# An encoder layer on one core: attention's last units write the out-projection's operand directly, rows are scaled in place, and the second pass loads in order on the sync queue

## The chip, the cores and the metric

The kernel runs on one core of a Trainium2 chip. The metric is the device time of one execution in microseconds (us). Three executions of the kernel before gave 2356.87, 2357.80 and 2357.84 us; the median is 2357.8. One more execution was recorded by the profiler: it took 2354.58 us, and the span of its recorded instructions is 2352.8 us, so 1.8 us lie outside the span.

## The reference

One layer on 2048 tokens plus 16 meta tokens, width 1024, all float32:

```python
hn = rms_norm(h, g_mix)
q, k, v, u = split(hn @ w_in)                  # 4 query heads, 2 key/value heads of 128; u is 512 wide
q, k = rope(rms_norm(q, g_q)), rope(rms_norm(k, g_k))
attn = softmax(q k^T / sqrt(128)) v            # every token sees every token
four = real(fft2(u per group of 128)) @ w_fourier
h = h + concat(rms_norm(attn), rms_norm(four)) @ w_out
h = h + relu(rms_norm(h) @ w_up)^2 @ w_down    # 1024 -> 4096 -> 1024
return rms_norm(h, g_final)[:, 16:]
```

## The kernel before

**Precision.** Every product of float32 matrices is made from three matmuls in a reduced type (`mm3`, lines 80 to 82): each operand is split into a high and a low part, high by high, high by low, low by high. A split is one cast on ACT (line 70) and one subtraction on DVE (line 71).

**Order of the work.** The program is written as generators. A scheduler turns it into one instruction order for each engine, and each engine runs its own order and waits on semaphores where an operand comes from another. The queue of SP (sync engine) and the queue of POOL (GpSimd) start the transfers, each in its own order: a transfer that has to wait holds up all that stand behind it in that queue.

**Stages.** First the in-projection, norms, rope and the first half of the Fourier transform. Then attention (about 327 to 1003 us of the span): 16 units, each 256 tokens by one key/value group with its two query heads. A unit's queries `q` are loaded by `start` (line 728) on the POOL queue, where the keys `kt` (line 704) and values `vn` (line 713) are loaded as well. A unit ends by splitting its output into `ohl` and storing the parts to the buffer `o_d` in device memory (line 853).

**Out-projection.** `out_a(b)` (from line 1009) does a block of 512 tokens: it loads the block's attention output from `o_d` into the operand `at` (line 1032), multiplies it with the weights into PSUM tiles `poa`, adds the result to the rows `h` (line 1042), squares them for the norm of the MLP (`hj`, line 1043) and stores them to `h_d` (line 1049). Four row tiles of 128 tokens make a block. Blocks 0 to 2 run in the shadow of attention, block 3 after it.

**Flip.** `flip(b)` (line 1052) makes the MLP's operand of a block: it scales the four row tiles by their norm into copies `m` (line 1057, 16 copies of 128 by 256 for a block), transposes these on TensorE into `pmt` (line 1062), applies the gain (`mt`, line 1064) and stores to `m_d`.

**MLP.** Two passes of 1024 tokens. Each pass is an up product and a down product in the seven-product scheme of Strassen and Winograd: operands are combined to seven forms, taken in the order "1265734" (`ORDER`). In the up pass one operand is `bf` (the seven forms of the tokens, which stay for the pass) and the other the weights' forms `wuh`, `wul` (`up_weights`, from line 1097), built from `R` (line 1104) for each of eight groups; a form is 24 matmuls per group. The results go through relu and square to `s_d`. In the down pass there are four groups of seven forms of 48 matmuls; tokens `ah`, `al` come from `s_d`, weights `bh`, `bl` from `w_down`. Both operands go through rings of tiles: `ar` (5 raw tiles), `a` (8), `b` (10).

**Between the stages.** After block 2 of the out-projection the program splits forms "1" and "2" of the first pass (blocks 0 and 1 of tokens), runs block 3 of the out-projection with the flip of block 2 between its parts, then the flip of block 3, then the other five forms. The second pass' forms are prepared during the first up pass (`forms_ahead`) and stored to `f_d`; they come back as seven transfers `bf<-f_d` of 2 MB (line 1536), four on POOL's queue behind the two weight loads `R`, three on SP's behind the stores of the first pass' output (line 1403).

Of the kernel before, what the change touches and what calls it, by code (L numbers as in the profile page):

```python
# [19 lines left out]
P = 128  # L20
# [6 lines left out]
NQ = 4  # L27
# [24 lines left out]
A_BUFS = 6  # L52
# [83 lines left out]
def encoder_block(ctx: ExitStack, tc: tile.TileContext, x, meta, w_in, w_f,  # L136
# [580 lines left out]
    sqs = {}  # L717

    def attention():
# [5 lines left out]
        def start(u):  # L725
            b, g = units[u]
            q = ap.tile([P, 2, 2, 256], R32, name=f"q_{u}", tag="q", bufs=2)
            nc.gpsimd.dma_start(q, q_d[b][:, :, 2 * g:2 * g + 2])
            q = q.rearrange("p l h n -> p l (h n)")
            state[u] = dict(q=(q[:, 0], q[:, 1]), S=[], k=KV["k", u])  # L730
# [107 lines left out]
        def finish(u):  # L838
# [11 lines left out]
            hl = ap2.tile([P, 2, 512], R32, name=f"ohl_{u}", tag="ohl", bufs=1)  # L850
            split(hl[:, 0], hl[:, 1], O)
            for e in range(2):
                nc.sync.dma_start(o_d[b // 2][:, e, 2 * g:2 * g + 2, c],
                                  f32v(hl[:, e]).rearrange("p (h n) -> p h n", h=2))
# [158 lines left out]
    def out_a(b):  # L1013
# [15 lines left out]
        A = ey.tile([P, 2, NQ, 512], R32, name=f"at_{b}", tag=f"e{b % 2}")  # L1029
        for k in range(NQ):  # L1030
            for e in range(2):
                nc.sync.dma_start(f32v(A[:, e, k]), o_d[b][:, e, k])
        MS[b] = ms = []
        for t in range(T):
# [14 lines left out]
            nc.sync.dma_start(h_d[2 * b0 + t], hs[t])  # L1049

    def flip(b):

        hs, ms = H.pop(b), MS.pop(b)
        for kk in range(KT // 2):
            m = [a_tile(f"m_{b}_{i}_{kk}").rearrange("p (t e) -> p t e", t=2) for i in range(2)]
            for t in range(4):
                nc.scalar.activation(m[t // 2][:, t % 2], hs[t][:, kk * 256:(kk + 1) * 256], AF.Copy, scale=ms[t])
            for i in range(2):
                k = 2 * kk + i
                ps = bank(f"pmt_{b}_{k}")  # L1060
                for t in range(4):
                    nc.tensor.transpose(ps[:, t * P:(t + 1) * P], m[t // 2][:, t % 2, i * P:(i + 1) * P], ident)
                raw = a_tile(f"mt_{b}_{k}")
                nc.scalar.activation(raw, ps, AF.Copy, scale=c_mlp(k))
                nc.sync.dma_start(m_d[b][:, k], raw)
            yield
# [30 lines left out]
    def up_weights(p, sp):  # L1097

        sp_t = {}
        for g in range(8):  # L1100
            R = []
            for i in range(2):
                r = sp.tile([P, 4, 512], F32, name=f"R{i}_{p}_{g}", tag=f"R{i}")
                (nc.gpsimd if p and not g else nc.sync).dma_start(r, w_up[i * 512:(i + 1) * 512, g * 512:(g + 1) * 512].rearrange("(k p) f -> p k f", p=P))
                R.append(r)
# [4 lines left out]
            def form(name, src):  # L1110
                hi, lo = (sp.tile([P, 4, 256], R32, name=f"wu{e}{name}_{p}_{g}", tag="wu" + e, bufs=WU_BUFS) for e in "hl")
                split(hi, lo, src)
                return hi, lo

            yield form("1", a11)
            yield form("2", a12)
# [11 lines left out]

    def bf_tile(pool, name, **kw):
        t = pool.tile([P, 2, 4, 512], R32, name="bf" + name, **kw)  # L1130
        BF[name] = [[t[:, e, k] for k in range(4)] for e in range(2)]
        return t

    def b_form(pool, name, src, **kw):

        t = bf_tile(pool, name, **kw)
        for c in (slice(0, 2), slice(2, 4)):
            split(t[:, 0, c], t[:, 1, c], src[:, c])
# [5 lines left out]
    def forms_ahead(lf):  # L1144

        for k, i in itertools.product(range(4), range(2)):
            r, c = {}, slice(i * 256, i * 256 + 256)
            for n, b, kk in (("11", 2, k), ("21", 2, k + 4), ("12", 3, k), ("22", 3, k + 4)):
                r[n] = lf.tile([P, 256], F32, name=f"lr{n}_{k}_{i}", tag="lr" + n)
                nc.sync.dma_start(r[n], m_d[b][:, kk, c])  # L1150

            def keep(name, src):
                t = lf.tile([P, 2, 256], R32, name=f"lf{name}_{k}_{i}", tag="lf", bufs=2)
                split(t[:, 0], t[:, 1], src)
                nc.sync.dma_start(f_d[name][:, :, k, c], f32v(t))

            sub = lambda d, a, b: nc.vector.tensor_tensor(r[d], r[a], r[b], op=ALU.subtract)
            keep("1", r["11"])
            yield
            keep("2", r["21"])  # L1160
            yield
            sub("11", "12", "11")
            keep("5", r["11"])
            yield
            sub("11", "22", "11")
            keep("6", r["11"])
            yield
            sub("12", "22", "12")
            keep("7", r["12"])
            yield  # L1170
            keep("3", r["22"])
            yield
            sub("21", "21", "11")
            keep("4", r["21"])
# [75 lines left out]
    def first_down(p, sp, FIRST):  # L1250

        a = sp.tile([P, 4, 512], F32, name=f"a1_{p}", tag="R0")
        nc.sync.dma_start(a, s_d[0][:, 0])
        w = sp.tile([P, 4, 512], F32, name=f"d11_{p}", tag="R1")
# [3 lines left out]
        for h in range(2):  # L1258
            for x, r in (("a", a), ("b", w)):
                tags = ("us1", "us2") if h and x == "b" else ("wuh", "wul")  # L1260
                hi, lo = (sp.tile([P, 2, 512], R32, name=f"{x}{e}1_{p}_{h}", tag=t, bufs=WU_BUFS if t in ("wuh", "wul") else 1)
                          for e, t in zip("hl", tags))
# [4 lines left out]
    def down_pass(p, sp, FIRST, hs):  # L1267
# [3 lines left out]
        for i, j in ((1, 1), (2, 1), (1, 2), (2, 2)):  # L1271
            pass
        own, RING = {}, {"a": (dn, 8)}

# [371 lines left out]
```

## Time and profile before

| what | value |
|---|---|
| median of three runs | 2357.8 us |
| the profiled execution | 2354.58 us, span 2352.8 us |
| TensorE busy (PE) | 2258.5 us, 96% of the span |
| VectorE (DVE) | 1694.7 us, 72% |
| ScalarE (ACT) | 1190.2 us, 51% |
| GpSimd (POOL) | 234.7 us, 10% |
| mean granted TensorE clock | 0.981 |
| attention | about 327 to 1003 us |
| between attention and the first up pass | about 1003 to 1115 us |
| first up pass, first down pass | to about 1387 us, to 1699 us |
| second up pass, second down pass | from 1719 to about 2044 us, to the end |

TensorE is busy in nearly all of the span, so what matters is where it is idle (about 94 us) and where its granted clock is below one. The view of waits names, for each engine, the instruction that waited and what released it; the timeline shows one wait at its place; the windows give the busy time of every engine and the granted clock for a stretch.

### The profile page before, as it was taken

How to read it: one execution, taken by the hardware profiler on the slowest of the kernel's cores; microseconds unless marked ns; L12 is line 12 of the kernel's file. 1: busy time of each engine (PE TensorE's matmuls, PEld its weight loads, DVE VectorE, ACT ScalarE, POOL GpSimd, SP SyncE). 2: the span in 40 equal slices, each digit the busy share in tenths (PEclk: the TensorE clock that was granted, in tenths of full speed). 3: DMA queues.
4: the chain of work that ended last, by engine and by line, in shares of the span. 5: the costliest groups of instructions: out<-in, count | busy, mean ns of one | idle time of the engine just before them, and what ended most of it. 6: DMA issues, size and time to landing. Idle time of an engine off the chain costs nothing.

```text
span 2352.8 us, 28180 instructions
## 1 busy us (share of the span) xinstructions
PE 2258.5 (96%) x10238; PEld 1786.2 (76%) x10238; DVE 1694.7 (72%) x2250; ACT 1190.2 (51%) x2045; POOL 234.7 (10%) x275
## 2 busy tenths in 40 slices
PE   9999989999999999967999999999879999999998
PEld 7889877766666666655888878888758888788887
DVE  5434669999998988845767659778635556597786
ACT  6333346656555657646656544324435555443244
POOL 1212120013232021100000020000100000200000
PEclk9999999999999999988999999999989999999999
DMA  6333142133343544354776486444274444864442
GB/s 205 89 91 100 54 146 78 50 121 110 112 135 119 179 130 144 134 207 148 243 245 223 167 311 217 145 149 135 99 321 170 140 156 159 304 216 147 147 135 81
DMA packets 192908, 368.47 MB, mean 157 GB/s; under 512 B 15856, under 2 KB 74864, under 8 KB 191104
## 3 DMA queue, kind: packets, MB, share of 16 engines
q1 hardware_dynamic: 172320, 304.84, 38.6%
q0 software_dynamic: 20304, 61.56, 8.0%
q8 instruction: 81, 1.33, 0.2%
q14 instruction: 59, 0.48, 0.1%
q10 hardware_dynamic: 144, 0.26, 0.0%
HBM read 236.28 MB, written 130.32 MB: 156 GB/s over the span
## 4 chain that ended last, share of the span: by engine, by line
PE 79%; DVE 7%; DMA 7%; ACT 3%; issue 2%; POOL 1%; SPq 0%; POOLq 0%; DVEq 0%; ACTq 0%
PE o L836 8%; PE dx L81 5%; PE dx L80 5%; PE dx L82 5%; PE dy L82 4%; PE dy L80 4%; PE dy L81 4%; PE ux L82 3%; PE ux L80 3%; PE ux L81 3%; PE uy L81 2%; PE uy L80 2%; PE uy L82 2%; PE s L80 2%; PE s L82 2%
## 5 line engine op out<-in xcount | busy, mean ns | idle before, releaser
L836 PE MATMUL o<-S,vn 128*128 128x512 f32 x512 | 244.2, 596 | 2.5 <-ACT S L828 1.9
L70 ACT CAST ah<-a 128x1024 fp32r<-128x1024 f32 x112 | 117.1, 1049 | 236.8 <-issue 122.8
L80 PE MATMUL ux<-bf,wuh 128*128 128x512 f32 x512 | 202.4, 395 | 29.2 <-DMA bf<-f_d 19.8
L767 ACT COPY S<-s 128x512 f32<-128x512 f32 x256 | 146.6, 585 | 111.4 <-PE s L82 91.9
L80 PE MATMUL dx<-bh,ah 128*128 128x512 f32 x512 | 200.1, 391 | 2.8 <-ACT bh L70 2.6
L81 PE MATMUL dx<-bl,ah 128*128 128x512 f32 x512 | 199.8, 390 | 2.1 <-DVE bl L71 2.1
L81 PE MATMUL ux<-bf,wuh 128*128 128x512 f32 x512 | 201.7, 394 | 0.0
L82 PE MATMUL ux<-bf,wul 128*128 128x512 f32 x512 | 201.5, 394 | 0.0
L82 PE MATMUL dx<-bh,al 128*128 128x512 f32 x512 | 199.4, 389 | 0.1
L80 PE MATMUL uy<-bf,wuh 128*128 128x512 f32 x384 | 151.1, 394 | 14.7 <-ACT bf L70 11.7
L827 DVE TENSOR_TENSOR S<-S,mb 128x1024 f32<-128x1024 f32 x128 | 155.7, 1232 | 12.0 <-ACT mb L798 11.9
L828 ACT ACTIVATE S<-S 128x1024 f32<-128x1024 f32 x128 | 135.1, 1063 | 43.7 <-DVE S L827 42.6
L80 PE MATMUL s<-q,kt 128*128 128x512 f32 (+1 forms) x272 | 146.1, 537 | 11.1 <-DMA q<-q_d 9.7
L80 PE MATMUL dy<-bh,ah 128*128 128x512 f32 (+1 forms) x388 | 151.9, 391 | 4.2 <-ACT ah L70 4.2
L71 DVE TENSOR_TENSOR al<-a,ah 128x1024 fp32r<-128x1024 f32 x112 | 136.2, 1223 | 25.9 <-ACT ah L70 25.1
L82 PE MATMUL dy<-bh,al 128*128 128x512 f32 (+1 forms) x388 | 151.6, 391 | 0.4 <-DVE al L71 0.4
L81 PE MATMUL uy<-bf,wuh 128*128 128x512 f32 x384 | 150.9, 393 | 1.1 <-DVE bf L71 1.1
L81 PE MATMUL dy<-bl,ah 128*128 128x512 f32 (+1 forms) x388 | 151.6, 391 | 0.0
L82 PE MATMUL uy<-bf,wul 128*128 128x512 f32 x384 | 150.7, 392 | 0.0
L836 PEld LDWEIGHTS o<-S,vn 128*128 128x128 f32 x512 | 92.1, 189 | 69.7 <-issue 56.4
L80 PEld LDWEIGHTS ux<-bf,wuh 128*128 128x128 f32 x512 | 97.8, 191 | 50.7 <-ACT wuh L70 20.2
L71 DVE TENSOR_TENSOR bl<-d,bh 128x1024 fp32r<-128x1024 f32 x96 | 117.2, 1222 | 26.0 <-ACT bh L70 25.8
(292 smaller groups left out, 5521.0 us busy)
## 6 DMA issues: line engine op xcount, KB each, us to landing
a<-s_d SPq DMA_DIRECT2D x84, 512.0 KB, 3.7
s_d<-s SPq DMA_DIRECT2D x128, 256.0 KB, 2.1
R<-in_w_up_dram SPq DMA_DIRECT2D x30, 1024.0 KB, 5.4
d<-in_w_down_dram SPq DMA_DIRECT2D x52, 512.0 KB, 5.0
s_d<-c SPq DMA_DIRECT2D x96, 256.0 KB, 2.5
f_d<-lf SPq DMA_DIRECT2D x56, 256.0 KB, 2.7
a<-s_d POOLq DMA_DIRECT2D x24, 512.0 KB, 5.6
x<-in_x_dram SPq DMA_DIRECT2D x16, 512.0 KB, 4.8
```

Source lines behind the costliest of these rows:

```text
L70: self.high = nc.scalar.copy(hi, src)
L71: self.low = nc.vector.tensor_tensor(lo, src, f32v(hi), op=ALU.subtract)
L80: nc.tensor.matmul(out, a[0], b[0], start=first, stop=False, skip_group_check=chain)
L81: nc.tensor.matmul(out, a[0], b[1], start=False, stop=False, skip_group_check=chain)
L82: nc.tensor.matmul(out, a[1], b[0], start=False, stop=last, skip_group_check=chain)
L767: nc.scalar.copy(S[:, i % 2], ps)
L827: nc.vector.tensor_tensor(S, S, mb, op=ALU.subtract)
L828: nc.scalar.activation(p, S, AF.Exp, scale=ISQ)
L836: nc.tensor.matmul(s["O"], v[:, 2 * j % 4 + e], p[:, e], start=i + e == 1, stop=False)
```

## The change

- The queries of unit 0 are loaded first on the POOL queue, ahead of the keys (`q0`), and handed to `start`, which now runs before the loads of the values.
- The last two units (`u >= len(units) - 2`: heads 0 and 1 of tokens 1536 to 2047) split their output straight into their place in the operand `at` of block 3 (`a_operand`). Only the other two heads of that block come from `o_d`. As program text the block's operand is opened by these units, ahead of `out_a(3)`.
- The rows are scaled in place (`scale_row`, one 128 by 1024 instruction on ACT per row tile) instead of into copies; the transposes of `flip` read `h` itself. Row tile `t-1` is scaled after row tile `t` has been multiplied, and after its store to `h_d`, which reads the unscaled rows; the last one at the start of `flip`. `A_BUFS` goes from 6 to 5.
- `out_a(3)` is opened ahead of the first up pass' pools; forms "1" and "2" keep their place in the program text; forms "7", "3" and "4" of the first pass are made in steps beside the first group's products (`later_forms`); `forms_ahead` follows them there and uses one area of memory.
- The down pass' memory is laid out by hand (`place`). In the first pass the rings have 4 raw tiles (`ar`) and 8 tiles (`b`); in the second 5 and 10 as before. The form "4" of the last group splits its weights to tiles of its own.
- In the second pass, the first weights come as two transfers `we` of 0.5 MB into tiles of the ring `ar` while the first down pass runs, and forms "1" and "2" of group 0 are split from them (`AHEAD`). All seven `bf` and the two `R` are on the SP queue. The stores of the first pass' output go to the POOL queue.

The core of the diff:

```diff
-A_BUFS = 6
+A_BUFS = 5
...
+    def a_operand(b, heads):
+        if b not in AT:
+            A = AT[b] = ey.tile([P, 2, NQ, 512], R32, name=f"at_{b}", tag=f"e{b % 2}")
+            for k in heads:
+                for e in range(2):
+                    nc.sync.dma_start(f32v(A[:, e, k]), o_d[b][:, e, k])
+        return AT[b]
...
+            if u >= len(units) - 2:
+                A = a_operand(3, (2, 3))
+                split(A[:, 0, 2 * g:2 * g + 2, c], A[:, 1, 2 * g:2 * g + 2, c], O.rearrange("p (h n) -> p h n", h=2))
+            else:
+                hl = ap2.tile([P, 2, 512], R32, name=f"ohl_{u}", tag="ohl", bufs=1)
...
+        q0 = load_q(0)
         for c in range(4):
             loads("k", 0, c)
+        start(0, q0)
         for c in range(5):
             loads("v", 0, c)
-        start(0)
...
             nc.sync.dma_start(h_d[2 * b0 + t], hs[t])
+            if t:
+                scale_row(b, t - 1)
+
+    def scale_row(b, t):
+        nc.scalar.activation(H[b][t], H[b][t], AF.Copy, scale=MS[b][t])
 
     def flip(b):
-        for kk in range(KT // 2):
-            m = [a_tile(f"m_{b}_{i}_{kk}").rearrange("p (t e) -> p t e", t=2) for i in range(2)]
+        scale_row(b, 3)
+        yield
+        hs = H.pop(b)
+        for k in range(KT):
+            ps = bank(f"pmt_{b}_{k}")
             for t in range(4):
-                nc.scalar.activation(m[t // 2][:, t % 2], hs[t][:, kk * 256:(kk + 1) * 256], AF.Copy, scale=ms[t])
...
+                nc.tensor.transpose(ps[:, t * P:(t + 1) * P], hs[t][:, k * P:(k + 1) * P], ident)
...
-                (nc.gpsimd if p and not g else nc.sync).dma_start(r, w_up[i * 512:(i + 1) * 512, g * 512:(g + 1) * 512].rearrange("(k p) f -> p k f", p=P))
+                nc.sync.dma_start(r, w_up[i * 512:(i + 1) * 512, g * 512:(g + 1) * 512].rearrange("(k p) f -> p k f", p=P))
...
+        a_bufs, b_bufs = (5, 10) if p else (4, 8)
...
+                if p == 0 and g == 3:
+                    early = [dn.tile([P, 4, 256], F32, name=f"we{i}", tag="ar", bufs=a_bufs) for i in range(2)]
+                    for i, r in enumerate(early):
+                        nc.sync.dma_start(r, w_up[i * 512:(i + 1) * 512, :256].rearrange("(k p) f -> p k f", p=P))
                 yield form("4", t4)
+            if p == 0:
+                for name, r in zip("12", early):
+                    AHEAD.append(wu_form(f"{name}_1_0", r))
...
-                eng = nc.scalar if final_pass and t == 7 and w is z else nc.sync
+                eng = nc.gpsimd if not final_pass else nc.scalar if t == 7 and w is z else nc.sync
...
+    def later_forms():
+        minus(b11, b12, b11)
+        b_split("5", b11)
+        minus(b11, b22, b11)
+        b_split("6", b11)
+        minus(b21, b21, b11)
+        yield
+        minus(b12, b22, b12)
+        b_split("7", b12)
+        yield
...
-        (nc.gpsimd if name in "1265" else nc.sync).dma_start(f32v(t), f_d[name])
+    nc.sync.dma_start(f32v(BT["1"]), f_d["1"])
+    nc.sync.dma_start(f32v(BT["2"]), f_d["2"])
     ready.append(next(UW))
+    for name in "65734":
+        nc.sync.dma_start(f32v(BT[name]), f_d[name])
```

**TensorE after attention.** `pas` is the sum of squares for the norm of block 3 (its two rows end block 2's part of the order), `poa` the out-projection, `uy` the up product's form "2" of group 0, `bf` its tokens. Before:

```order
3859 L82 MATMUL poa_1_3_8874<-woh_1_7244,at_8450 128x512
3860 L1024 MATMUL pas_8956<-ones,sq_8049 128x1 x2
3861 L1024 MATMUL pas_8956<-ones,sq_8356 128x1 x2
3862 L80 MATMUL uy_0_0_0_9411<-bf_8943,wuh_0_0_8920 128x512
3863 L80 MATMUL uy_0_0_1_9424<-bf_8943,wuh_0_0_8920 128x512
3864 L81 MATMUL uy_0_0_0_9411<-bf_8943,wuh_0_0_8920 128x512
```

The same place in the order of the change:

```order
3859 L1079 MATMUL pmt_7_8851<-ident,h_3_7798 128x128
3860 L1042 MATMUL pas_8877<-ones,sq_8003 128x1 x2
3861 L1042 MATMUL pas_8877<-ones,sq_8322 128x1 x2
3862 L80 MATMUL poa_0_0_8889<-woh_0_7202,at_8627 128x512
3863 L81 MATMUL poa_0_0_8889<-wol_0_7203,at_8627 128x512
3864 L82 MATMUL poa_0_0_8889<-woh_0_7202,at_8627 128x512
```

Before, the up product's form "2" came first after attention and the out-projection's block 3 stood behind it; now block 3 comes first, and form "2" follows at row 3990, after the block's 96 matmuls and the 32 transposes of `flip(2)`.

**ScalarE in block 1's part of the order** (still beside attention): `hj` is the square of row tile 0's second half, `mt` the flip's gain, `S` and `mb` belong to attention's units, `h_1_0` is the row tile scaled in place.

```order
774 L1058 ACTIVATE hj_1_0_1_7882,hss_1_0_7820<-h_1_0_7792 128x512
775 L1081 ACTIVATE mt_0_0_7889<-pmt_0_0_7884,cols_94 128x512
776 L780 COPY S_14_0_7905<-s_14_0_7901 128x512
777 L811 COPY mb_13_7907<-pd_m13_7908 128x512
778 L1069 ACTIVATE h_1_0_7792<-h_1_0_7792,rs_m2_7963 128x1024
779 L780 COPY S_14_0_7905<-s_14_1_7917 128x512
```

Three instructions stand between the square and the scaling; the scaling waits for the store of the same rows to `h_d`, and attention's next copy `S` stands behind it.

**The SP queue around the second pass' start.** `bf` 133 to 139 are the forms "1", "2", "6", "5", "7", "3", "4"; `R` and `we` are weights; `hs` are the first pass' output rows. Before:

```order
563 L1403 DMA out_dram<-hs_0_11830 128x512 x8
564 L1403 DMA out_dram<-hs_1_12092 128x512 x2
565 L1536 DMA bf_14267<-f_d_137 128x4096
566 L1403 DMA out_dram<-hs_1_12092 128x512 x6
567 L1536 DMA bf_14269<-f_d_138 128x4096
568 L1536 DMA bf_14271<-f_d_139 128x4096
```

The change:

```order
556 L1413 DMA we_13877<-in_w_up_dram 128x4x256
557 L1413 DMA we_13878<-in_w_up_dram 128x4x256
558 L1612 DMA bf_14104<-f_d_137 128x4096
559 L1608 DMA bf_14100<-f_d_133 128x4096
560 L1609 DMA bf_14101<-f_d_134 128x4096
561 L1128 DMA R_1_0_14109<-in_w_up_dram 128x4x512
562 L1128 DMA R_1_0_14111<-in_w_up_dram 128x4x512
563 L1612 DMA bf_14102<-f_d_135 128x4096
564 L1612 DMA bf_14103<-f_d_136 128x4096
565 L1612 DMA bf_14105<-f_d_138 128x4096
566 L1612 DMA bf_14106<-f_d_139 128x4096
```

The output stores have left this queue for POOL's, and the loads of forms "1", "2", "6" and "5" and of the two `R` have come from there; form "7" (137) stands first, ahead of form "1" (133). It goes to the memory of the first four output row tiles (`hs_0`) and waits until their eight stores have landed.

More of the change, by code (lines that the diff above doesn't have):

```diff
@@ L849, in finish @@
             c = slice(b % 2 * 256, b % 2 * 256 + 256)
[L850 to L854, printed above, removed]
+            if u >= len(units) - 2:
[3 more added lines that the diff above has]
+                hl = ap2.tile([P, 2, 512], R32, name=f"ohl_{u}", tag="ohl", bufs=1)
+                split(hl[:, 0], hl[:, 1], O)
+                for e in range(2):
+                    nc.sync.dma_start(o_d[b // 2][:, e, 2 * g:2 * g + 2, c],
+                                      f32v(hl[:, e]).rearrange("p (h n) -> p h n", h=2))
             nc.scalar.square(O, O)
@@ L1028, in out_a @@
         ra = rstd_of(mp, ss[:, :T], T, 512, "a")
[L1029 to L1032, printed above, removed]
+        A = a_operand(b, range(NQ))
         MS[b] = ms = []
@@ L1095, in left, with wu_tile, wu_form, up_weights @@
         return Lines(tc.alloc_tile_pool(name=name, bufs=1, reuse_waits="tile"), small)
[L1097 to L1099 removed]
+    def wu_tile(name, tag, shape=(4, 256)):
+        return wup.tile([P, *shape], R32, name=name, tag=tag, bufs=WU_BUFS)
+    def wu_form(name, src):
+        hi, lo = (wu_tile(f"wu{e}{name}", "wu" + e) for e in "hl")
+        split(hi, lo, src)
+        return hi, lo
+    def up_weights(p, sp, spr):
         for g in range(8):
@@ L1108, in up_weights @@
             a12, a22 = R[1][:, :, :256], R[1][:, :, 256:]
[L1110 to L1116, printed above, removed]
+            form = lambda name, src: wu_form(f"{name}_{p}_{g}", src)
+            if g or not p:
+                yield form("1", a11)
+                yield form("2", a12)
             nc.vector.tensor_tensor(s1, a21, a22, op=ALU.add)
@@ L1142, in minus, with forms_ahead, load, keep @@
             nc.vector.tensor_tensor(dst[:, c], a[:, c], b[:, c], op=ALU.subtract)
-    def forms_ahead(lf):
-        for k, i in itertools.product(range(4), range(2)):
-            r, c = {}, slice(i * 256, i * 256 + 256)
-            for n, b, kk in (("11", 2, k), ("21", 2, k + 4), ("12", 3, k), ("22", 3, k + 4)):
[L1149 to L1160, printed above, removed]
+    def forms_ahead():
+        area = u_tile("lf", 1).rearrange("p k n -> p (k n)")
+        items = list(itertools.product(range(4), range(2)))
+        r, turn = {}, [0]
+        def load(k, i):
+            for n, b, kk in (("11", 2, k), ("21", 2, k + 4), ("12", 3, k), ("22", 3, k + 4)):
+                r[n] = area[:, 256 * len(r):256 * len(r) + 256] if n not in r else r[n]
+                nc.sync.dma_start(r[n], m_d[b][:, kk, i * 256:i * 256 + 256])
+        def keep(name, src, k, i):
+            t = area[:, 1024 + 512 * turn[0]:1536 + 512 * turn[0]].rearrange("p (e n) -> p e n", e=2)
+            turn[0] ^= 1
+            split(t[:, 0].bitcast(R32), t[:, 1].bitcast(R32), src)
+            nc.sync.dma_start(f_d[name][:, :, k, i * 256:i * 256 + 256], t)
+        sub = lambda d, a, b: nc.vector.tensor_tensor(r[d], r[a], r[b], op=ALU.subtract)
+        load(*items[0])
+        yield
+        for at, it in enumerate(items):
+            keep("1", r["11"], *it)
+            keep("2", r["21"], *it)
@@ L1519, in encoder_block @@
-    rs_.release()
+    def later_forms():
[7 more added lines that the diff above has]
+        b_split("7", b12)
+        yield
+        for name, r, slots in (("3", b22, (2, 0)), ("4", b21, (3, 4))):
+            t = BT[name] = [u_tile(f"bf{name}{e}", i, R32) for e, i in zip("hl", slots)]
+            BF[name] = [[v[:, k] for k in range(4)] for v in t]
+            for c in (slice(0, 2), slice(2, 4)):
+                split(t[0][:, c], t[1][:, c], r[:, c])
+            yield
```

136 lines of the change are left out of this document (74 added, 62 removed).

## The prediction

> **What bounds the kernel now.** First the page: which engine is busy, and which chain ends last.
>
> ```profile
> span 2352.8 us, 28180 instructions
> PE 2258.5 (96%) x10238; PEld 1786.2 (76%) x10238; DVE 1694.7 (72%) x2250; ACT 1190.2 (51%) x2045; POOL 234.7 (10%) x275
> ```
>
> TensorE (PE) is the bound: 2352.8 - 2258.5 = 94.3 us are all that it idles. So I read its waits, longest first, and ask of each edit which of them it takes away.
>
> ```profile
> PE ux L80 <- DMA bf<-f_d: 19.8, 1, 19.8
> PE pmt L1062 <- ACT m L1057: 15.8, 9, 2.3
> PE uy L80 <- ACT bf L70: 11.7, 1, 11.7
> PE s L80 <- DMA q<-q_d: 9.7, 1, 9.7
> PE ux L80 <- ACT p L1217: 7.8, 1, 7.8
> PE dy L80 <- ACT ah L70: 4.2, 1, 4.2
> PE dx L80 <- ACT bh L70: 2.6, 1, 2.6
> PE uy L80 <- DMA bf<-f_d: 2.6, 1, 2.6
> PE dx L81 <- DVE bl L71: 2.1, 1, 2.1
> PE ux L80 <- ACT c L1183: 1.6, 1, 1.6
> PE uy L81 <- DVE bf L71: 1.1, 1, 1.1
> ```
>
> These eleven make 79.0 of the 94.3 us, and they lie at five places: attention's start (`q`), the transition after attention (`pmt`, `uy` from ACT and DVE, `ux` from `p`: 11.7 + 1.1 + 7.8 and 15.8, of which 15.2 there), the first down pass' start (`dx`), the second up pass' start (`bf<-f_d`, `c`) and the second down pass' start (`dy`). A wait costs more than its length, as the timeline at attention's start shows:
>
> ```profile
> 337.22 0.76 PE L80 MATMUL s<-q,kt 128*128 128x512 f32 x1 [9.67 <-DMA q<-q_d]
> 337.79 0.63 PE L81 MATMUL s<-q,kt 128*128 128x512 f32 x1
> 338.21 0.63 PE L82 MATMUL s<-q,kt 128*128 128x512 f32 x1
> ...
> 343.31 0.40 PE L82 MATMUL s<-q,kt 128*128 128x512 f32 x1
> 343.55 0.39 PE L80 MATMUL s<-q,kt 128*128 128x512 f32 x1
> ```
>
> After the idle time matmuls start 0.42 us apart, later 0.24 (0.227 over longer stretches). The slow spacing lasts some 10 matmuls here: 2.1 us on top of 9.7.
>
> **Term 1: queries first, -11.8 us.** POOL's queue before, and the fourth `kt`'s time from issue to landing:
>
> ```profile
> 314.14 2.37 POOL L704 DMA_DIRECT2D kt<-k_d  x3
> 326.11 0.71 POOL L704 DMA_DIRECT2D kt<-k_d  x1 [9.61 <-DMA k_d<-kt]
> 329.51 0.73 POOL L728 DMA_DIRECT2D q<-q_d  x1
> kt<-k_d POOLq DMA_DIRECT2D x1, 608.0 KB, 4.4
> ```
>
> The load of `q` stood behind the fourth `kt`, which waited 9.61 us for a store, and behind five loads of values. Now it is issued at about 314, and even if it takes the 337.2 - 329.5 = 7.7 us that it took between its issue and the first score, it is there before PE is free at 327.55. The fourth `kt` is next: issued at 326.11, it is needed after twelve score tiles of three matmuls, 36 x 0.227 = 8.2 us later, by when the trace's 4.4 us for it have passed. Bounds: 0 (something else holds the first score) to 9.7 + 2.1 = 11.8. I take 11.8: nothing else of the first scores is missing.
>
> **Term 2: the transition, -32 us.** How much there is:
>
> ```profile
> 1003.00:1110.00 107.00, 71.29 (x293) 55.29 (x294) 54.03 (x74) 58.59 (x108) 3.72 (x6) 0.82 0.46 167
> 1015.00:1023.00 8.00, 6.62 (x19) 4.85 (x20) 8.00 (x8) 1.22 (x2) 0.00 (x0) 0.62 0.63 249
> 1041.00:1047.00 6.00, 5.46 (x20) 4.15 (x20) 0.21 (x1) 2.70 (x6) 0.00 (x0) 0.72 0.23 85
> 1066.00:1072.00 6.00, 3.94 (x16) 2.67 (x16) 0.85 (x2) 4.99 (x12) 0.00 (x0) 0.50 0.54 197
> 1072.00:1080.00 8.00, 6.75 (x22) 5.46 (x23) 1.77 (x5) 4.96 (x11) 0.00 (x0) 0.56 0.52 182
> ```
>
> (windows: PE, weight loads, DVE, ACT, POOL busy, then the granted clock.) PE idles 107 - 71.3 = 35.7 us, and busy time at a low clock, 6.62 x 0.38 + 5.46 x 0.28 + 3.94 x 0.50 + 6.75 x 0.44, adds 9.0: 44.7 us at most can go. What held it was a round trip: the last unit's parts went to `o_d` and back, so PE's order put form "2" ahead of block 3, and form "2" waited for `b` and its casts:
>
> ```profile
> at<-o_d SPq DMA_DIRECT2D x4, 256.0 KB, 13.2
> b<-m_d SPq DMA_DIRECT2D x4, 1024.0 KB, 10.1
> L1057 ACT ACTIVATE m<-h,rs_m 128x256 f32<-128x256 f32 x32 | 13.6, 497 | 0.0
> L70 ACT CAST ah<-a 128x1024 fp32r<-128x1024 f32 x112 | 117.1, 1049 | 236.8 <-issue 122.8
> ```
>
> Now block 3 reads parts that lie in its operand, 96 matmuls (96 x 0.227 = 21.8 us) run at once, and `b`, the casts and the flip of block 2 have that cover. The transposes no longer alternate with copies of 0.5 us: a row tile is scaled once, 1.05 us by the cast of the same 128 by 1024, sixteen for 64, 16.8 us for 31.8 in all.
>
> What is late next: the rows of block 3 take the memory of block 1's, so their loads now wait for `flip(1)`'s last transposes, at about 1007, with `b`'s 4 MB behind them on SP's queue (10.1 us from issue to landing); the first addition to `h` then starts near 1012, some three row halves (12 x 0.227 = 2.7 us each) behind PE. Counted along the new orders with such durations, ACT has about 40 us and DVE about 36 of work by 1041 for block 3, a flip and four forms, so both are nearly full, and block 3's last row has to be added, stored (2.9 us, term 3) and scaled (1.05) before `flip(3)`'s fourth transposes. I count three stalls of 2 to 4 us and 3 us of low clock after them: 12 of the 44.7 stay. Bounds: 15 won (only the round trip of `o_d` and its low clock) to 41.
>
> **Term 3: scaling in place inside attention, +4 us.** The scaling waits for the store of the same rows, and attention's copies stand behind it on ACT.
>
> ```profile
> h_d<-h SPq DMA_DIRECT2D x8, 512.0 KB, 2.9
> ```
>
> From the finished row, the store lands after 0.3 + 2.9 us; ACT meanwhile has the square (0.8) and, at the tightest, three instructions of 0.6: 3.2 - 2.6 = 0.6 us of waiting, or 2 where the store takes half as long again. For twelve row tiles that is 7 to 24 us of ACT, and PE, which has out-projection matmuls between the scores, sees part: bounds 0 to 20, I take 4, near the lower end, since ACT is busy for half of the span only.
>
> **Term 4: the second pass' start, -11 us.** SP's and POOL's queues and PE before:
>
> ```profile
> 1690.43 5.78 SPq L1403 DMA_DIRECT2D out_dram<-hs  x5
> 1696.43 0.33 SPq L1536 DMA_DIRECT2D bf<-f_d  x1
> ```
>
> ```profile
> 1699.09 0.81 POOL L1104 DMA_DIRECT2D R<-in_w_up_dram  x1 [0.32 <-PE dx L81]
> 1701.74 0.80 POOL L1104 DMA_DIRECT2D R<-in_w_up_dram  x1 [0.23 <-issue]
> 1702.53 0.55 POOL L1536 DMA_DIRECT2D bf<-f_d  x1
> ```
>
> ```profile
> 1718.97 0.76 PE L80 MATMUL ux<-bf,wuh 128*128 128x512 f32 x1 [19.84 <-DMA bf<-f_d]
> 1699.00:1730.00 31.00, 11.16 (x39) 8.93 (x39) 11.94 (x13) 7.31 (x10) 4.30 (x7) 0.67 1.00 409
> ```
>
> Form "1"'s `bf` was issued at 1702.53, behind both `R`, while SP's form "7" and the stores shared the engines (all busy, 409 GB/s). Now the weights of "1" and "2" are made early, and `bf` "1" is second on SP behind form "7". Before, that left at 1696.43 behind the same eight stores; by POOL's queue I give them a us more, so both leave at about 1697.5: 4.2 MB at 0.41 MB a us land at 1707.8, with a share for the other stores 1709. PE is free at 1699.1: 10 us idle instead of 19.8. Behind it `bf` "2" is in time, but `R` is now later: with 8.4 MB ahead and stores beside, about 1721, then two sums and a split, four instructions of a little over 1 us, against forms "1" and "2", which end near 1723: 3 us, in place of 2.6 + 1.6. Gain 9.8 + 1.2 = 11. Bounds: 3 (`R` and the stores late) to 24 (form "7" leaves early and `bf` "1" is there at 1699).
>
> [...]
>
> **Terms 5 and 6: the two down passes' starts, -3 and -1 us.** Idle there: 2.6 + 2.1 and 4.2 us, plus about 2.5 of slow matmuls each. The new layout lets the first pass' weights load before the last group's end, but form "2"'s tiles now wait for form "1"'s last matmul, and two casts of 1.05 us and a subtraction follow: 2 to 3 us with some slow matmuls come back. Bounds +4 to -7 together. The shorter rings (`ar` 4, `b` 8) I cost at nothing: `a` already has 8 tiles, two forms, and in 290 us of down pass PE never waited:
>
> ```profile
> 1400.00:1690.00 290.00, 290.00 (x1281) 240.15 (x1280) 235.52 (x271) 113.66 (x134) 8.51 (x16) 1.00 0.46 152
> ```
>
> A form is 10.9 us, with 235.5 / 290 x 10.9 = 8.9 us of DVE's work for a later one: 2 us of slack are the cover.
>
> **Sum.** -11.8 - 32 + 4 - 11 - 3 - 1 = -54.8 us. The profiled execution of 2354.6 would take 2299.8; the median of the runs shown stands 3.2 above it, so 2303.
>
> **Rivals.**
> - *The transition refills (0.20).* ACT and DVE or the late rows bound it, and only 15 to 20 us go, term 3 being near 10: 2303 + 15 + 6 = 2324. For it: 59 us of ACT and 54 of DVE in those 107 us, packed into 75. Against: most of it waited for PE before.
> - *Nothing new in the way (0.18).* Form "7" leaves early, so `bf` "1" and `R` come 8 us sooner, and 40 us go in the transition: 2303 - 8 - 8 = 2287. Against it: eight stores in front.
> - *The queries change nothing (0.10).* Engines were full until 337; a store of `q` or the first copies might hold the scores: 2303 + 11.8 = 2315.
> - *The rings stall (0.07), slower.* If a form's splits can't start until two forms back has ended, each of 25 forms of the first down pass waits; with 3 us at each and low clock after, 75 to 110 us come, 2378 or more. It decides from 55 / 25 = 2.2 us a form. For it: DVE's 2 us of slack. Against it: `a`'s ring of the same length.
>
> **How the numbers follow.** Forecast 0.45: 2303, its own range 2293 to 2314. The rivals at 2287, 2315 and 2324 belong to the 8 in 10, so the range is 2280 to 2332; outside lie the rings and sums of bounds. A change can be told here from about 0.2%, 4.7 us. Faster: 0.45 + 0.20 + 0.18 + 0.10 less 0.03 for cases that add up badly = 0.90; same 0.03; slower 0.07.
>
> **What would show it.** The wait for `q<-q_d` is gone and attention starts at about 327.6. `poa` follows `pas` without a gap, and group 0's last product ends some 32 us nearer to attention's end, with waits of a few us at `pmt` on ACT. In the second pass the wait for `bf<-f_d` is about 10 us. PE waits for ACT's `S` in attention show term 3. I would be wrong if `dx` or `dy` waited at every form, or if ACT or SP set the transition.

## The result

The changed kernel took 2297.0 us (median of four runs, 2295.1 to 2301.7) beside 2357.3 before (2356.6 to 2357.8). The ratio is 0.9747, with a 95% interval of 0.9730 to 0.9764. The forecast was 2303 with a range of 2280 to 2332, so the direction was right and the time lies in the range. The profiled execution took 2295.14 us with a span of 2293.4, 59.4 us less than the 2352.8 before.

From the page and the view of TensorE's waits after the change, longest first (three dots stand for rows left out):

```profile
span 2293.4 us, 28136 instructions
PE 2242.5 (98%) x10238; PEld 1775.1 (77%) x10238; DVE 1692.7 (74%) x2250; ACT 1177.4 (51%) x1997; POOL 247.2 (11%) x285
PE ux L80 <- DMA bf<-f_d: 18.7, 2, 12.6
PE dy L80 <- ACT ah L70: 4.9, 2, 2.8
PE o L849 <- ACT S L841: 3.4, 5, 1.5
PE s L80 <- ACT S L780: 2.5, 7, 0.6
PE dx L80 <- DVE hs L1485: 2.5, 1, 2.5
PE dx L80 <- ACT ah L70: 1.7, 2, 0.9
...
PE dx L81 <- DVE bl L71: 1.4, 1, 1.4
...
PE pmt L1079 <- ACT h L1069: 0.7, 1, 0.7
```

TensorE idles 50.9 us instead of 94.3, which is 43.4 of the 59.4 us. The other 16.0 us are its busy time, 2258.5 to 2242.5: the same 10238 instructions, fewer of them at the low clock (the mean granted clock was 0.981 and is 0.994). The waits for `q`, for `m` and for the casts of `bf` are gone from the list. One long entry is left, the loads at the second pass' start.

The windows show what became of the transition. Each row runs from the end of `pas` to the last product of group 0 of the first up pass, before and after the change. The columns are the stretch and its length, then the busy time of PE, weight loads, DVE, ACT and POOL, then the granted clock, the share of the transfer engines and their GB/s:

```profile
1003.70:1119.60 115.90, 80.23 (x329) 62.69 (x330) 61.65 (x83) 64.21 (x116) 3.72 (x6) 0.84 0.48 174
995.50:1065.80 70.30, 68.56 (x330) 55.84 (x330) 58.25 (x75) 54.42 (x85) 7.23 (x6) 1.00 0.73 271
```

TensorE's work is the same in both rows: out-projection block 3, both flips and group 0, 264 matmuls and 64 transposes (the counts take in a neighbour or two at the ends). It took 115.9 us at a mean clock of 0.84 and now takes 70.3 at full clock. Of these 45.6 us, 33.9 were idle time (35.7 to 1.7) and 11.7 busy time. DVE and ACT do in 70 us nearly as much as they did in 116, and TensorE waits for them for only 1.4 us.

Stage by stage, from the times at which TensorE's work of each stage starts and ends in the two profiled executions:

| stretch | before, us | after, us | difference | predicted |
|---|---|---|---|---|
| start to the first score | 337.2 | 327.2 | -10.0 | -9.7, and -2.1 of low clock in the next row |
| first score to the end of block 2's order (`pas`) | 666.4 | 668.2 | +1.8 | -2.1 + 4 |
| `pas` to the end of the first up pass | 383.3 | 338.2 | -45.1 | -32 |
| to the end of the first down pass | 312.2 | 311.3 | -0.8 | -3 |
| to the first product of the second up pass | 19.8 | 12.6 | -7.2 | -11 for both rows |
| second up pass | 313.7 | 315.1 | +1.4 | |
| second down pass and the end of the span | 320.3 | 320.9 | +0.6 | -1 |

The second up pass before ends, and its second down pass begins, at about 2033 us, not at about 2044.

The two largest errors have opposite signs: the transition gave 13 us more than forecast, and the pass starts 9 us less. That the total came out this near is in part luck.

### The profile page after: what moved, and what is told of

Its sections match the earlier page's. It is cut to its first block, busy times and chain, and to the rows that moved or that the text cites. A ratio compares the mean times of both kernels' runs of the same rounds, so it can differ in the third digit from the quotient of the medians.

```text
span 2293.4 us, 28136 instructions
## 1 busy us (share of the span) xinstructions
PE 2242.5 (98%) x10238; PEld 1775.1 (77%) x10238; DVE 1692.7 (74%) x2250; ACT 1177.4 (51%) x1997; POOL 247.2 (11%) x285
## 4 chain that ended last, share of the span: by engine, by line
PE 79%; DVE 8%; DMA 6%; ACT 3%; issue 2%; POOL 1%; SPq 1%; POOLq 0%; DVEq 0%; ACTq 0%
PE o L849 6%; PE dx L80 5%; PE dx L82 5%; PE dx L81 5%; PE dy L82 4%; PE dy L80 4%; PE dy L81 4%; PE ux L80 4%; PE ux L81 4%; PE ux L82 4%; PE uy L80 3%; PE uy L82 3%; PE uy L81 3%; PE s L80 2%; PE s L82 2%
## 5 line engine op out<-in xcount | busy, mean ns | idle before, releaser
L80 PE MATMUL ux<-bf,wuh 128*128 128x512 f32 x448 | 176.8, 395 | 18.8 <-DMA bf<-f_d 18.7
L81 PE MATMUL ux<-bf,wuh 128*128 128x512 f32 x448 | 175.8, 392 | 0.0
L82 PE MATMUL ux<-bf,wul 128*128 128x512 f32 x448 | 175.7, 392 | 0.0
L840 DVE TENSOR_TENSOR S<-S,mb 128x1024 f32<-128x1024 f32 x128 | 155.4, 1229 | 11.8 <-ACT mb L811 11.7
L80 PE MATMUL uy<-bf,wuh 128*128 128x512 f32 x320 | 125.2, 391 | 0.3 <-ACT wuh L70 0.3
L82 PE MATMUL uy<-bf,wul 128*128 128x512 f32 x320 | 124.7, 390 | 0.7 <-DVE wul L71 0.7
L81 PE MATMUL uy<-bf,wuh 128*128 128x512 f32 x320 | 124.9, 390 | 0.0
L786 DVE TENSOR_TENSOR M<-M,S 128x1024 f32<-128x1024 f32 x96 | 117.8, 1227 | 9.1 <-ACT S L780 8.1
```

The costliest lines, as they stand in the source:

```text
L80: nc.tensor.matmul(out, a[0], b[0], start=first, stop=False, skip_group_check=chain)
L81: nc.tensor.matmul(out, a[0], b[1], start=False, stop=False, skip_group_check=chain)
L82: nc.tensor.matmul(out, a[1], b[0], start=False, stop=last, skip_group_check=chain)
L786: nc.vector.tensor_tensor(M, M, S, op=ALU.max)
L840: nc.vector.tensor_tensor(S, S, mb, op=ALU.subtract)
```

## The experiments

Each kernel below is the changed kernel with one edit, or with those that are named. Times are medians of four runs; the ratio to the kernel before, with its interval, is given for each. "Profiled" is the one execution with a trace, and the lengths of stretches are from it; for the change itself it is 1.9 us below the median.

**The round trip of the last units' parts.** The last two units store to `o_d` again, and block 3 loads all heads from there.

```diff
-            if u >= len(units) - 2:
+            if u >= len(units):
```

> The changed kernel, with the last two units writing their parts to device memory again and block 3 of the out-projection loading all four heads from there; all else as changed. The order of TensorE still has block 3 right behind attention. Theory A, the round trip was what held the transition: the parts are stored, land after 2 us, and are loaded in 3 to 13 us, so TensorE waits 5 to 15 us before block 3, with 3 us of low clock after it, and the profiled time rises from 2295 by 8 to 18 us, to 2303 to 2313. Theory B, the order of the work and the scaling in place did it, and the direct write adds little: a wait under 4 us, 2295 to 2299.

Measured: 2311.4 us, ratio 0.9806 (0.9791 to 0.9820). In the timeline of TensorE behind attention there is one long wait:

```profile
1010.88 0.76 PE L80 MATMUL poa<-woh,at 128*128 128x512 f32 x1 [14.90 <-DMA at<-o_d]
```

From `pas` to the end of the first up pass it takes 354.0 us instead of 338.2. Theory A holds: with this order of work the direct write is worth 15.8 us there, 14.4 us by the medians.

**The copies.** The rows are scaled into copies of 256 columns as before.

```diff
-A_BUFS = 5
+A_BUFS = 6
...
-            if t:
-                scale_row(b, t - 1)
...
-                nc.tensor.transpose(ps[:, t * P:(t + 1) * P], hs[t][:, k * P:(k + 1) * P], ident)
...
+                nc.scalar.activation(m[t // 2][:, t % 2], hs[t][:, kk * 256:(kk + 1) * 256], AF.Copy, scale=ms[t])
...
+                    nc.tensor.transpose(ps[:, t * P:(t + 1) * P], m[t // 2][:, t % 2, i * P:(i + 1) * P], ident)
```

> The changed kernel, with the rows scaled into copies of 256 columns again, as before the change (and one work tile more, as before); all else as changed. The order of TensorE then mixes out-projection, transposes and the first up product in the transition. Theory A, the scaling in place carries the transposes' part of the gain: the waits of the transposes for the copies come back, some 15 us with 5 us of low clock, while the 3 us that TensorE waits more in attention than before the change go away; the profiled time rises from 2295 by 10 to 18 us, to 2305 to 2313. Theory B, with block 3's parts at hand the copies are hidden by the other products: within 4 us of 2295, and under 4 us of waits of transposes.

Measured: 2307.5 us, ratio 0.9794 (0.9775 to 0.9812). From its view of waits:

```profile
PE pmt L1077 <- ACT m L1072: 10.3, 8, 2.8
...
PE o L849 <- ACT S L841: 1.9, 3, 1.0
...
PE s L80 <- ACT S L780: 0.9, 2, 0.5
```

The transition, again from `pas` to the end of the first up pass, takes 351.4 us, 13.2 more than with scaling in place. Attention, from the first score to `pas`, takes 664.4 us, 3.8 less. Both halves of theory A are there: scaling in place gains 13.2 us behind attention and loses 3.8 in it. By the medians it is worth 10.5 us in all.

**Both undone.** The round trip and the copies are back together.

> The changed kernel, with the round trip of the last two units' parts and the copies of the rows both back, so that of the transition's changes only the order of the program (block 3 of the out-projection opened first, forms 3, 4 and 7 made late) and the layout stay. Alone, the round trip cost 16 us and the copies 11 us. Theory A, each holds another place and they add up: 2295 + 16 + 11 = 2322, with 13 to 16 us of wait for the parts and 8 to 12 for the copies; the order itself is then worth the rest of the transition's 45 us, some 15 us. Theory B, they overlap (the copies of block 2 are made while TensorE waits for the parts): 2312 to 2317, and the order is worth over 20 us.

Measured: 2318.8 us, ratio 0.9833 (0.9818 to 0.9848); the profiled execution took 2315.5, the lowest of the four. The waits of its transition, from the view of the whole execution (0.6 us of the first row lie in attention):

```profile
PE pmt L1077 <- ACT m L1072: 7.5, 7, 2.0
PE poa L80 <- DMA at<-o_d: 5.5, 1, 5.5
...
PE uy L80 <- ACT bf L70: 2.9, 2, 1.8
...
PE uy L81 <- DVE bf L71: 1.6, 1, 1.6
```

The transition takes 361.1 us, 22.9 more than the change, while the two edits alone sum to 15.8 + 13.2 = 29.0. So they overlap by 6 us there, and theory B is nearer; by the medians (14.4 + 10.5 against 21.8) the overlap is 3 us and the result lies between the two theories. The wait for `at` is 5.5 us here and was 14.9 with scaling in place. Scaling in place puts the transposes for the last three tiles of `flip(1)` right ahead of `pas`, and on SP's queue their stores to `m_d` and the four loads of `h` then stand ahead of the loads of `at`: the first of these leaves at 1002.0 us there, and at 991.8 us here. That this is the whole of the 9 us was not tried by itself.

**The place of block 3 in the program.** `out_a(3)` is no longer opened ahead of the weights of the first up pass.

```diff
     last_out = out_a(3)
-    next(last_out)
```

> The changed kernel, with block 3 of the out-projection no longer opened ahead of the first up pass' weights, as in the program before the change; the direct write and the scaling in place stay. On TensorE the up product's form 2 then stands between the block's second and third row tile instead of behind the block. Theory A, with the parts at hand the order of the program matters little: 2295 to 2299, under 4 us of new waits. Theory B, form 2 comes before its operand is ready (b loaded and split) and holds the out-projection behind it: 5 us or more of wait for its split, with low clock 2302 to 2312.

Measured: 2307.1 us, ratio 0.9786 (0.9766 to 0.9807); the runs spread from 2302.0 to 2312.4 us, and the profiled one is the slowest. The timeline of TensorE in its transition:

```profile
1010.08 1.22 PE L80 MATMUL uy<-bf,wuh 128*128 128x512 f32 x2 [4.38 <-ACT bf L70]
...
1037.17 1.12 PE L1079 MATMUL pmt<-ident,h 128*128 128x128 f32 x6 [0.65 <-ACT mt L1081]
...
1038.68 0.73 PE L80 MATMUL uy<-bf,wuh 128*128 128x512 f32 x2 [0.39 <-ACT bf L70]
```

The up product's form "2" now stands behind three of block 3's eight row halves and waits for its cast, with the rest of block 3 behind it. The work from `pas` to the end of group 0 takes 79.5 us instead of 70.3: 4.3 us more of idle time and 4.9 us more of busy time, at a granted clock of 0.94. To the end of the first up pass it is 351.8 us, 13.6 more, of which 2.6 are a wait for `p` far behind the transition. Theory B. By the medians the place in the program is worth 10.1 us, about as much as the scaling in place, and less than the direct write.

**The late forms.** Forms "7", "3" and "4" are made ahead of the first up products.

```diff
     rest = later_forms()
-    next(rest)
+    drain(rest)
```

> The changed kernel, with forms 7, 3 and 4 of the first pass made ahead of the first up products instead of in steps beside them. Theory A, the late forms carry part of the gain: before the change TensorE waited 7.8 us in the first up pass for a copy that stood behind those splits on ScalarE; 5 to 8 us come back, with low clock 2301 to 2306. Theory B, without the other stalls there is time for all seven: within 3 us of 2295.

Measured: 2299.7 us, ratio 0.9753 (0.9738 to 0.9769), against 0.9747 for the change: no difference that these runs tell. The wait for the copy `p` of 7.8 us doesn't come back; 2.3 us more are waited for `h` at the last flip. Theory B.

**All four undone.** The round trip, the copies, block 3 opened behind the weights and the forms made ahead are back together.

> The changed kernel with all four edits of the transition undone: round trip, copies, block 3 opened behind, forms ahead. From the end of attention to the end of the first up pass the kernel before took 383.3 us, the change 338.2, the change without direct write and scaling in place 361.1. Theory A, these four edits are all of the transition's 45 us: 380 to 385 us for that stretch, 2337 to 2343 in all. Theory B, the new memory layout or the smaller set of work tiles has a share of its own: under 378 us, below 2335.

Measured: 2329.9 us, ratio 0.9880 (0.9862 to 0.9898). The order on TensorE again has form "2" first behind `pas`, and the waits are those of the kernel before, but one:

```profile
PE pmt L1077 <- ACT m L1072: 13.6, 9, 2.3
PE uy L80 <- ACT bf L70: 12.1, 2, 11.0
...
PE uy L81 <- DVE bf L71: 1.8, 1, 1.8
```

The stretch takes 377.1 us and the whole less than 2335, as theory B has it, though by little: 38.9 of the 45.1 us are these four edits, 6.2 are not. What is missing from the waits is `ux` for `p`, 7.8 us before and 0.6 here. The remaining 6 us are about the size of that wait; what of the rest of the change (the memory of the forms, the place of `forms_ahead`) removed it, and whether it is all of them, stays open.

**The queries.** The load of unit 0's `q` stands behind keys and values again.

```diff
-        q0 = load_q(0)
         for c in range(4):
             loads("k", 0, c)
-        start(0, q0)
         for c in range(5):
             loads("v", 0, c)
+        start(0)
```

> The changed kernel, with the queries of unit 0 loaded behind the keys and values again; all else as changed. Theory A, the place in GpSimd's queue alone made the wait at attention's start: 9 to 10 us of wait for the queries come back with about 2 us of low clock, 2295 to 2305 to 2308 profiled. Theory B, the layout or the load of the transfer engines made it: under 3 us of wait, 2295 to 2299.

Measured: 2306.5 us, ratio 0.9786 (0.9770 to 0.9802), 9.5 us above the change by the medians and 11.3 by the profiled executions. The view of waits has one new row:

```profile
PE s L80 <- DMA q<-q_d: 9.8, 1, 9.8
```

Theory A: before the change this wait was 9.7 us.

**Scaling in place, a little later.** In blocks 0 to 2 a row tile's scaling stands behind the first square of the next row tile on ACT.

```diff
...
             if t:
-                scale_row(b, t - 1)
+                with tc.issue_after(j0) if b < 3 else nullcontext():
+                    scale_row(b, t - 1)
```

> The changed kernel, with the scaling in place of a row tile in blocks 0 to 2 put on ScalarE behind the first square of the next row tile, some 5 us later. In the changed kernel ScalarE waited there 14.2 us for the row's norm from GpSimd and 3.7 us for the store of the rows, and TensorE waited 8.2 us in attention against 5.3 before the change. Theory A, these waits of ScalarE are what lengthened attention by about 4 us: both waits fall under 4 us in sum, TensorE's waits in attention to about 5 us, and the time by 2 to 4 us. Theory B, ScalarE's waits lay in its idle time and the difference comes from other work in attention: TensorE's waits stay at 7 to 9 us and the time within 1 us.

Measured: 2291.5 us, ratio 0.9723 (0.9709 to 0.9738). ACT's waits at the scaling, from 780 us to the end of attention, in the change and then here:

```profile
ACT h L1069 <- POOL rs_m L192: 14.2, 6, 3.3
ACT h L1069 <- DMA h_d<-h: 3.7, 3, 1.4
```

```profile
ACT h L1071 <- POOL rs_m L192: 2.6, 2, 2.1
ACT h L1071 <- DMA h_d<-h: 0.6, 1, 0.6
```

17.9 us of ACT's waits become 3.2, attention takes 663.7 us instead of 668.2, and the span is 4.5 us shorter. Theory A, and by its own number: TensorE's waits in attention fall from 8.2 to 5.8 us. In the change the wait for the row's norm from GpSimd was four times that for the store. The edit takes both away together, so it does not tell what each is worth.

**Form "7" later in the queue.** Its load stands behind that of form "5" on SP.

```diff
-    for name in "65734":
-        nc.sync.dma_start(f32v(BT[name]), f_d[name])
+    for name in "65":
+        five = ins_of(nc.sync.dma_start(f32v(BT[name]), f_d[name]))
+    with tc.issue_after(five):
+        for name in "734":
+            nc.sync.dma_start(f32v(BT[name]), f_d[name])
```

> The changed kernel, with the load of form 7 (and 3 and 4) queued behind that of form 5 on SP, so that forms 1 and 2 and the two weight loads no longer stand behind the one that waits for eight output stores. In the changed kernel TensorE idles 12.6 us and 6.1 us here for the loads, and the low clock after them costs about 4 us. Theory A, the place in the queue sets it: form 1's load can leave at about 1626 us, when its memory has been read, 19 us before the first down pass ends, so both waits go to 0 to 2 us, and the profiled time falls from 2295 by 18 to 23 us, to about 2273. Theory B, the shared transfer engines set it (14.6 us from issue to landing for the 4 MB of two forms): the loads still take until some 10 us after the down pass, the first wait stays at 8 us or more, and the time falls by no more than 6 us, to about 2290.

Measured: 2284.4 us, ratio 0.9691 (0.9677 to 0.9706). SP's queue around the end of the first down pass, in the change and here:

```profile
1642.47 0.34 SPq L1612 DMA_DIRECT2D bf<-f_d  x1
1642.97 0.34 SPq L1608 DMA_DIRECT2D bf<-f_d  x1
```

```profile
1626.37 0.34 SPq L1608 DMA_DIRECT2D bf<-f_d  x1
1626.76 0.42 SPq L1609 DMA_DIRECT2D bf<-f_d  x1
1627.23 1.32 SPq L1128 DMA_DIRECT2D R<-in_w_up_dram  x2
```

Form "1" leaves 16.6 us earlier and both waits for forms (12.6 and 6.1 us) are gone: the place in the queue set them, as theory A has it. The gain is 11 us by the profiled executions (12.6 by the medians), though, not 18 to 23. Two things took the rest. The two loads of the weights `R` landed 21.2 and 27.1 us after they were issued, behind 4 MB of forms, and form "6" waited for them:

```profile
1660.89 0.74 PE L80 MATMUL ux<-bf,wuh 128*128 128x512 f32 x1 [4.99 <-ACT wuh L70]
```

And the second down pass took 3.7 us more, with a low clock at its start, 0.88 over 43 us (last section).

**Weights first.** With form "7" late and the scaling behind the square, both loads of `R` stand ahead of all forms on SP.

```diff
...
-    nc.sync.dma_start(f32v(BT["1"]), f_d["1"])
-    nc.sync.dma_start(f32v(BT["2"]), f_d["2"])
     ready.append(next(UW))
-    for name in "65734":
-        nc.sync.dma_start(f32v(BT[name]), f_d[name])
+    for name in "1265734":
+        with tc.issue_after(LAST[0]):
+            LAST[:] = [ins_of(nc.sync.dma_start(f32v(BT[name]), f_d[name]))]
```

> The changed kernel with both earlier edits (form 7 queued late on SP, scaling behind the next row's square) and the two weight loads R of the second pass ahead of all seven forms on SP. With form 7 late, the two waits for forms were gone but form 6's weights came 5.0 us late, since R landed 24 us after its issue, behind forms 1 and 2. Theory A, the order of the loads sets it: R can leave at about 1616 us, ten us ahead of form 1, so the 5.0 us go and the 4 us in attention too; from 2284 profiled to 2272 to 2276. Theory B, the transfer engines' rate sets it (forms 1, 2, 6 and the output stores are 10 MB, 25 us at 0.42 MB a us): the wait moves to form 2 or 6, 3 us or more of TensorE's waits stay between the passes, and the time is 2277 to 2281.

Measured: 2273.0 us, ratio 0.9640 (0.9625 to 0.9654), the fastest kernel of this study, 24 us below the change; of these, 5.5 us are what the later scaling gave alone and 12.6 what form "7" gave alone, by the medians. Its queue, and all that TensorE waits from 1630 to 1950 us:

```profile
1613.09 1.05 SPq L1132 DMA_DIRECT2D R<-in_w_up_dram  x2
1623.12 31.07 SPq L1615 DMA_DIRECT2D bf<-f_d  x7
```

```profile
PE ux L82 <- DVE wul L71: 0.7, 1, 0.7
PE ux L80 <- ACT p L1250: 0.4, 1, 0.4
```

Theory A: the second pass follows the first without a gap. The second up pass takes 307.1 us, where the kernel before took 313.7 and waited 19.8 ahead of it.

**The output stores.** The stores of the first pass' output are back on SP's queue.

```diff
-                eng = nc.gpsimd if not final_pass else nc.scalar if t == 7 and w is z else nc.sync
+                eng = nc.scalar if final_pass and t == 7 and w is z else nc.sync
```

> The changed kernel, with the stores of the first pass' output on SP's queue again, so that form 1's load stands behind the last of them (ready some 6 us after the down pass). Theory A, order within SP sets the second pass' start: form 1's load leaves 8 us later than the 1643 us of the changed kernel and the wait grows from 12.6 to 18 us or more; 2301 to 2306 in all. Theory B, the bytes set it (stores and loads share the engines on either queue): the wait grows by under 3 us, 2295 to 2299.

Measured: 2295.3 us, ratio 0.9737 (0.9721 to 0.9752): the same as the change. The two waits at the second pass' start:

```profile
1658.26 0.77 PE L80 MATMUL ux<-bf,wuh 128*128 128x512 f32 x1 [15.62 <-DMA bf<-f_d]
1674.09 0.50 PE L80 MATMUL ux<-bf,wuh 128*128 128x512 f32 x1 [3.11 <-ACT wuh L70]
```

15.6 + 3.1 against 12.6 + 6.1 us: the same 18.7. Form "1" leaves SP 4.3 us after the down pass has ended (1646.9 to 1642.6) instead of 2.0 us ahead of its end, but lands 11.2 us after that, not 14.5: form "7" left 7.0 us ahead of it here, and only 0.5 us ahead of it in the change, so less was in front. Form "6" can start 31.5 us after the down pass' end in both. Theory B, in the sum. The queue of the stores costs nothing here, where form "7" stands ahead of form "1": 2295.3 us beside 2297.0.

**The rings.** The second down pass gets the short rings of the first.

```diff
-        a_bufs, b_bufs = (5, 10) if p else (4, 8)
+        a_bufs, b_bufs = 4, 8
```

> The changed kernel, with the shorter rings of the first down pass (4 raw tiles, 8 weight tiles) in the second down pass as well, which has 5 and 10. Theory A, the splits keep two forms ahead with either length: the second down pass keeps its 321 us to within 2 us, no new waits at each form, 2293 to 2298 profiled. Theory B, a shorter ring stalls the splits at each of its 28 forms: 2 us or more each, the second down pass takes 30 us longer or more, 2325 or above.

Measured: 2299.4 us, ratio 0.9754 (0.9740 to 0.9769). The second down pass takes 322.4 us from its first product to the span's end instead of 320.9, and TensorE waits 1.8 us ahead of that product, where the change did not. Behind it stand three more waits in the first 35 us, 2.4, 2.8 and 2.5 us, and none at later forms. So theory A on the forms: no stall at each of them. The profiled execution, 2301.3 us, is 3 us above its range, and about 3 us are lost at the pass' start.

## Why the prediction was right

*Term 1, the queries (-11.8).* Right in mechanism and size: the first score came 10.0 us earlier, the low clock behind it is gone (0.63 from 337.0 to 343.5 us before, 1.00 from 327.2 to 340.0 now), and undoing the edit gave back 9.8 us of wait and 11.3 us in all (9.5 by the medians).

*Term 2, the transition (-32).* Right in direction, too small by 13 us. The idle time in the bound, 35.7 us, was read rightly; the low clock, 9.0 us from four windows, was 11.7 over all of this work. The step that failed is the last one, "I count three stalls of 2 to 4 us and 3 us of low clock after them: 12 of the 44.7 stay". What stayed were 1.7 us, most of it at the last flip and at the first group's weights, and no low clock (1.00 over the 70.3 us). The rows of block 3 were late as it said: the first addition to `h` started 7.2 us behind `pas`, three row halves behind TensorE. But ACT, which it gave about 40 us of work for block 3, a flip and four forms, was through with these at 1032.8 us, 37.3 us after `pas`, and busy for 28.7 of them (DVE 33.2, where it said about 36).

The step on the cause was wrong too, "so PE's order put form "2" ahead of block 3": with the round trip back, block 3 still came first. It was the place of `out_a(3)` in the program that let form "2" in, behind three row halves when undone alone, and first of all with the other three edits undone as well. The direct write, the scaling in place and that place carry 14.4, 10.5 and 10.1 us by the medians when undone alone, 15.8, 13.2 and 13.6 from `pas` to the end of the first up pass. All of them together, with the late forms, are 38.9 there, so they overlap a little.

*Term 3, scaling in place (+4).* The size was right, 3.8 us by the copies and 4.5 by the later scaling. The cause named was the smaller wait: late in attention ACT stood 3.7 us for the store and 14.2 us for the norm that GpSimd makes. No run parted the two.

*Term 4, the second pass (-11).* Too large by 5 us. The step "so both leave at about 1697.5", 1.6 us before the down pass' end, was near: they left 2.5 and 2.0 us before it. The first step that failed is the landing, "with a share for the other stores": form "1" landed 14.5 us after its issue and not 11.5. From 1642.4 to 1657.6 us the transfer engines moved 378 GB/s, 5.7 MB; that is 1.5 MB beside the two forms, and the share was 1.2 us, 0.5 MB. The stores of the last rows, on POOL's queue, landed in that time. The second is what it let form "6" wait for: it priced `R` at 3 us, but `R` had landed at 1671.4 us, and the wait of 6.1 us was for form "6"'s own load, which landed at 1676.3 and stands nowhere in the term.

The transfers of the two queues share the engines: from 1699.1 to 1719.0 us before, POOL's queue took 58.9% of the 16 engines' time and SP's 40.9%. For the waits it made no difference in the sum on which of the two the stores stand: 18.7 us on either. The order inside a queue counted for more: putting form "7" behind form "5" gave 11 us.

*Terms 5 and 6, the down passes' starts (-3 and -1).* They gave -0.8 and +0.6. In the first pass the two waits of 2.6 and 2.1 us are gone. In their place stand 0.9 us within form "1" and, as was said of form "2"'s tiles, 2.1 and 0.7 us at the start of form "2", with a clock of 0.71 over the 5.8 us from there. In the second pass four waits of 1.4, 0.9, 2.8 and 2.5 us took the place of 4.2 and 0.4. No run undid the layout or the early weights by themselves.

*The rivals.* "Nothing new in the way" was right on the transition and wrong on form "7", which did wait. The rings did not stall form by form, in either pass. "The transition refills" fell, and so did "the queries change nothing".

## What to carry to other kernels

In a queue that runs in order, a transfer that has to wait belongs behind all that could already go: moving one 2 MB load back by six places, and two 1 MB loads to the front, took TensorE's waits between the end of the first down pass and the end of the second up pass from 18.7 us to 1.1. Look at where a block is opened in the program, not only at its data path: an instruction whose operand comes late, standing ahead of work that could run, cost 10 us here, beside 14 us for the round trip through device memory. And price a wait with the low clock that follows it: 16 of the 59 us came from busy time.

## What was not expected

In these runs the same wait does not always lower the clock. At the start of the second down pass the changed kernel waited 1.4, 0.9, 2.8 and 2.5 us, the kernel with form "7" later 2.2, 0.6, 2.8 and 0.9 us. The windows of 43 us from that start, the change first:

```profile
1972.00:2015.00 43.00, 35.41 (x152) 27.73 (x151) 34.03 (x37) 19.35 (x23) 6.34 (x12) 1.00 0.75 275
```

```profile
1957.00:2000.00 43.00, 36.49 (x138) 28.36 (x137) 31.76 (x37) 17.52 (x21) 6.34 (x12) 0.88 0.71 262
```

With less idle time, 6.5 instead of 7.6 us, the clock was 0.88 and not 1.00, and the pass took 3.7 us more. Part of this goes with a longer wait. In three kernels the wait for the subtraction `bl` at the pass' start is 2.2 to 2.4 us (form "7" later, the output stores on SP, the short rings), and from the end of the second up pass to the span's end they take 323.9 to 324.4 us. With the short rings, matmuls start 0.43 us apart for 4.6 us behind this wait; in the change they start 0.23 us apart behind it. In the other kernels that wait is 1.4 us or less, and they take 319.1 to 321.0. But the wait of 2.8 us after it is the same in the change and with form "7" later, and the 8 us from its end are not, again with the change first:

```profile
1989.50:1997.50 8.00, 7.96 (x35) 6.62 (x36) 8.00 (x8) 2.70 (x3) 4.21 (x8) 1.00 0.59 205
```

```profile
1977.70:1985.70 8.00, 7.98 (x28) 6.42 (x29) 8.00 (x8) 2.74 (x3) 4.21 (x8) 0.79 0.59 202
```

Why a wait of one length lowers the clock in one kernel and not in the other is not shown: no run here moved a wait by itself. This puts a limit on comparing these kernels by a few us: the two second down passes differ by 3.7 us, with waits that differ by 1.1 us in sum.
